# A mixture-of-experts layer on one core: another way to the first expert pair's tokens

## The chip, the cores and the metric

The kernel runs on one core of a Trainium2 chip. The metric is the device time of one execution in microseconds (us). Five engines work from queues of their own: TensorE (PE in the profile, its weight loads PEld), VectorE (DVE), ScalarE (ACT), GpSimd (POOL) and SyncE (SP), which here only issues DMAs. A wait at the head of a queue holds all that stands behind it.

## The reference

512 tokens of width 2048 go through one decoder layer in f32: normalisation, two attention groups, an output projection, and a mixture of experts. Only the last part matters here:

```python
def hierarchical_moe(h, router_g, router_e, w_gate, w_up, w_down):
    """h (N,D). Top-1 expert group, then top-2 experts inside the group."""
    pg = jax.nn.softmax((h @ router_g).astype(jnp.float32), axis=-1)
    ...
    top_p, top_i = lax.top_k(jax.nn.softmax(le, axis=-1), EXPERT_TOPK)
    gate = g_w[:, None] * top_p / jnp.sum(top_p, axis=-1, keepdims=True)
    expert = g_idx[:, None] * EXPERTS_PER_GROUP + top_i.astype(jnp.int32)
    ...
        u = jax.nn.silu(xe @ w_gate[e]) * (xe @ w_up[e])
        return u @ w_down[e]
    ...
    return jnp.zeros_like(h).at[buf_tok].add(yb * buf_w[:, None].astype(h.dtype))
```

There are 32 experts; each has three matrices of 4 MB (2048 x 512). Every token goes to two of them.

## The kernel before

All code is unrolled, and each engine's instructions stand in the order in which the Python code writes them; nothing reorders them. The first half of the kernel (to about 900 us) is the attention and the output projection. Its last steps are in `main_o`: for the last column block (c = 3) each of four groups of 128 tokens (t) is summed (`add_up`), turned and squared (`turn`: the copy `x1T` and the sum of squares `jk`), and multiplied with the router's weights (`route`). `keep` stores a block of the result `x1` to `x1d` in DRAM. `rs` and `r2` are the norm of each token.

Then comes the routing, mostly on VectorE with tokens on the partitions: `lgt` are the router's results, `first_max` finds the group and the two experts, M holds one-hot rows over 32 experts, and the matmuls `pos` count for each token its place in each expert. `key` is 512 times the expert plus the place, `gt` the two gate weights. `make_row` turns a column of 128 x 4 numbers into a row over 512 tokens on all partitions (four matmuls into a PSUM bank and a copy by ScalarE to `rows` or `more`); keys, `r2` and the gates are needed in that form.

The experts go in 16 pairs; an expert has 64 places, so that a pair fills 128 partitions. `find` compares the rows of keys with the keys of a pair's 128 places, which gives the one-hot matrix oT, and by products with `toki` (token numbers, loaded by GpSimd's queue) and `rrow` the token's number and norm for each place. GpSimd then gathers the tokens from `x1d` into xg by an indirect DMA; a place without a token has a number beyond the table, and its row is left as it was (xg is cleared once). `normed` scales xg, `turn_x` turns a quarter of it (four transposes on TensorE, four activations with scale and bias on ScalarE) into xe. A pair then multiplies with w_gate (g, four quarters of 16 matmuls), w_up (u) and w_down (y); an expert's weights come as four loads a matrix. `combine` adds the results to the tokens in the next pair's time. `find` for pair n + 1 stands ahead of pair n's g.

What sets the order of the loads: all large tiles come from one pool of 23 buffers (`slot`), handed out in the order of the code. SyncE issues the loads in order; `load_to(n)` issues up to item n, and a load waits until its buffer's last reader is done. Ahead of the first pair `load_to(n_phase1 + 12)` is called, so that 12 expert weights have buffers ahead of `rows`, `more`, two xg and xe; a thirteenth takes the router's buffer, and the next ones those of the first pair's weights as g uses them.

Of the kernel before, what the change touches and what calls it, by code (L numbers as in the profile page):

```python
# [34 lines left out]
C_ID, C_US, C_CM, C_SK, C_EI, C_D8, C_D4 = 0, 128, 256, 384, 400, 432, 440  # L35
NC_ = 444
# [41 lines left out]
def tile_hybrid_layer(ctx: ExitStack, tc, A, out, dbg=None):  # L78
# [891 lines left out]
    def main_o(c, q, h, start, stop):  # L970
# [9 lines left out]
        for t in range(4):  # L980
# [7 lines left out]
            if (c, q, h) == (3, 3, 1):  # L988
                add_up(c, t, pm, V)
                if t:  # L990
                    turn(c, t - 1)
                if t > 1:
                    route(c, t - 2)
            yield
        if stop:
            if c == 3:
# [5 lines left out]
                keep(c)  # L1002
# [67 lines left out]
    load_to(n_phase1 + 12)  # L1070
# [54 lines left out]
    M = k2([P, 3, 4, 32], "M")  # L1125
    for i, oh in enumerate((oh1, oh2)):
        V.tensor_tensor(M[:, i].rearrange("p t (g e) -> p t g e", g=4),
                        ohg[:, :, :, None].to_broadcast([P, 4, 4, 8]),
                        oh[:, :, None, :].to_broadcast([P, 4, 4, 8]), op=OP.mult)
# [17 lines left out]
    rows = slot([P, 4, S], name="rows")  # L1147
    more = slot([P, 2, S], name="more")
    rrow, toki = more[:, 0], more[:, 1]
    G.dma_start(toki, A["toki"])  # L1150

    def make_row(dst, col):

        pb = bank("at", "rows")
        for t in range(4):
            mm(pb[:, 128 * t:128 * t + 128], col[:, t:t + 1].to_broadcast([P, P]), ident, True, True)
        act(dst, pb)

    make_row(rows[:, 0], key[:, 0])
    make_row(rows[:, 1], key[:, 1])  # L1160
    make_row(rrow, r2)
# [13 lines left out]
    xg = [slot([P, D], name=f"xg{i}") for i in range(2)]  # L1175
    for t in xg:
        G.memset(t, 0.0)


    def find(sk, xs):  # L1180


        oT = k2([P, S], "oT", F32R)
        g = sm.tile([P, 6], F32, name="gs", tag="gs", bufs=3)
        gi = sm.tile([P, 1], I32, name="gi", tag="gi", bufs=3)
        t1 = sm.tile([P, S], F32, name="t1", tag="tmp", bufs=3)
        V.tensor_scalar(t1, rows[:, 0], sk, None, op0=OP.is_equal)
        V.scalar_tensor_tensor(oT, rows[:, 1], sk, t1, op0=OP.is_equal, op1=OP.add)
# [22 lines left out]
    def turn_x(xe, xs, c):  # L1211
# [45 lines left out]
    def need(i, k, e, c):  # L1257
        load_to(base + i + 1 + AH)
# [225 lines left out]
```

## Time and profile before

| | us |
|---|---|
| median of three executions | 1916.92 (1915.95 to 1920.93) |
| the profiled execution, its own time | 1916.49 |
| its span, first to last instruction | 1914.7 |
| TensorE busy | 1749.3 (91%) |
| VectorE busy | 973.1 (51%) |
| ScalarE busy | 602.1 (31%) |
| GpSimd busy | 393.2 (21%) |

The span is shown in 40 slices of 47.9 us, and the DMA engines' rate in them changes in the 20th: 374 GB/s in the 19th, 183 in the 20th, then 415 to 420 in each slice up to the 39th. A busy TensorE is no sign of its being the limit, since its matmuls count as busy while they stand in its pipeline. The chain that ended last is DMA for 42% of the span, w_u, w_d and w_g in turn.

### The profile page before, as it was taken

How to read it: one execution, taken by the hardware profiler on the slowest of the kernel's cores; microseconds unless marked ns; L12 is line 12 of the kernel's file. 1: busy time of each engine (PE TensorE's matmuls, PEld its weight loads, DVE VectorE, ACT ScalarE, POOL GpSimd, SP SyncE). 2: the span in 40 equal slices, each digit the busy share in tenths (PEclk: the TensorE clock that was granted, in tenths of full speed). 3: DMA queues.
4: the chain of work that ended last, by engine and by line, in shares of the span. 5: the costliest groups of instructions: out<-in, count | busy, mean ns of one | idle time of the engine just before them, and what ended most of it. 6: DMA issues, size and time to landing. Idle time of an engine off the chain costs nothing.

```text
span 1914.7 us, 21344 instructions
## 1 busy us (share of the span) xinstructions
PE 1749.3 (91%) x8098; PEld 982.9 (51%) x8098; DVE 973.1 (51%) x1473; ACT 602.1 (31%) x1138; POOL 393.2 (21%) x307
## 2 busy tenths in 40 slices
PE   4999999988899998897799999999999999999997
PEld 1777777765676676785433333333334333333333
DVE  6889722489846578768223243323333343323335
ACT  3655444554457534343221101211021101211020
POOL 3533311342436336665000000000000000000000
PEclk9999999999999999999899999999999999999999
DMA  9878312323235647679499999999999999999997
GB/s 350 278 267 293 132 66 88 132 89 110 89 105 225 222 158 272 255 287 374 183 420 419 419 419 419 419 419 420 419 419 419 419 420 419 419 419 419 419 415 284
DMA packets 136426, 585.06 MB, mean 306 GB/s; under 512 B 10760, under 2 KB 43696, under 8 KB 78976
## 3 DMA queue, kind: packets, MB, share of 16 engines
q1 hardware_dynamic: 132240, 569.09, 75.4%
q0 software_dynamic: 4080, 14.57, 2.1%
q8 instruction: 65, 1.06, 0.2%
q14 instruction: 41, 0.34, 0.0%
HBM read 583.60 MB, written 8.40 MB: 309 GB/s over the span
## 4 chain that ended last, share of the span: by engine, by line
DMA 42%; PE 8%; DVE 1%; issue 0%; ACT 0%; SPq 0%; DVEq 0%
DMA w_u<-in_w_up 17%; DMA w_d<-in_w_down 13%; DMA w_g<-in_w_gate 12%; PE y L103 3%; PE u L103 3%; PE g L103 1%; PE cb L103 1%; DVE x L1237 1%; PE ga L1215 1%; DMA xg<-x1d,gi 0%; DVE xg L1209 0%; DVE u L1272 0%; PE uT L1278 0%; DVE yt L1227 0%; DVE yL L1229 0%
## 5 line engine op out<-in xcount | busy, mean ns | idle before, releaser
L103 PE MATMUL u<-w_u,xe 128*64 128x512 f32 x1024 | 272.8, 617 | 29.9 <-DMA w_u<-in_w_up 29.2
L1237 DVE TENSOR_TENSOR x<-cb,x 128x512 f32<-128x512 f32 x256 | 157.2, 680 | 194.5 <-PE cb L103 194.5
L103 PE MATMUL g<-w_g,xe 128*64 128x512 f32 x1024 | 240.5, 597 | 14.5 <-DMA w_g<-in_w_gate 14.4
L103 PE MATMUL y<-w_d,uT 128*64 128x512 f32 x1024 | 236.9, 600 | 0.7 <-ACT uT L100 0.7
L1193 POOL DMA_INDIRECT xg<-x1d,gi x16 | 16.1, 1004 | 874.4 <-DVE t L1196 632.7
L282 POOL TENSOR_TENSOR accv<-accv,w_m_None 128x768 f32<-128x768 f32 (+2 forms) x62 | 153.0, 2468 | 207.7 <-ACT w_m_None L100 123.6
L103 PEld LDWEIGHTS u<-w_u,xe 128*64 128x64 f32 x1024 | 80.8, 140 | 211.0 <-issue 138.8
L103 PEld LDWEIGHTS g<-w_g,xe 128*64 128x64 f32 x1024 | 76.1, 137 | 168.0 <-issue 133.4
L1227 DVE SCALAR_TENSOR_TENSOR yt<-y,gs,accv 128x512 f32<-128x512 f32 x64 | 47.8, 747 | 202.4 <-PE y L103 202.4
L280 DVE SCALAR_TENSOR_TENSOR accv<-w_m_None,sil,accv 128x1280 f32<-128x1280 f32 (+2 forms) x62 | 134.8, 2174 | 5.9 <-issue 5.4
L100 ACT ACTIVATE xe<-ga,modc 128x128 f32<-128x128 f32 x256 | 94.5, 465 | 119.5 <-PE y L103 92.6
L103 PEld LDWEIGHTS y<-w_d,uT 128*64 128x64 f32 x1024 | 66.6, 136 | 116.0 <-issue 107.9
L100 ACT ACTIVATE uT<-uT 128x512 f32<-128x512 f32 x16 | 9.6, 598 | 358.7 <-PE uT L1278 358.7
L103 PE MATMUL cb<-yH,oT 128*128 128x512 f32 x256 | 107.8, 421 | 0.9 <-DVE x L1237 0.9
L100 ACT ACTIVATE yH<-yt 128x512 fp32r<-128x512 f32 x64 | 40.3, 630 | 204.6 <-DVE yt L1227 121.5
L103 PE MATMUL cb<-yL,oT 128*128 128x512 f32 x256 | 101.1, 395 | 0.0
L1229 DVE TENSOR_TENSOR yL<-yt,yH 128x512 fp32r<-128x512 f32 x64 | 44.3, 692 | 110.4 <-PE g L103 58.1
L394 DVE TENSOR_TENSOR hl<-w_O,hl 128x1024 fp32r<-128x1024 f32 x32 | 67.8, 2121 | 42.3 <-ACT hl L100 31.7
L1272 DVE TENSOR_TENSOR u<-sg,u 128x512 f32<-128x512 f32 x16 | 11.0, 688 | 127.9 <-PE u L103 127.9
L282 POOL TENSOR_TENSOR acc<-acc,w_m 128x160 f32<-128x160 f32 x105 | 61.2, 583 | 70.6 <-ACT w_m L100 62.9
L103 PEld LDWEIGHTS cb<-yH,oT 128*128 128x128 f32 x256 | 48.2, 188 | 50.0 <-issue 39.1
L1215 PEld LDWEIGHTS ga<-cst,xg 128*128 128x128 f32 x256 | 36.8, 210 | 64.3 <-issue 43.5
(413 smaller groups left out, 3168.7 us busy)
## 6 DMA issues: line engine op xcount, KB each, us to landing
w_g<-in_w_gate SPq DMA_DIRECT2D x128, 1024.0 KB, 19.9
w_u<-in_w_up SPq DMA_DIRECT2D x128, 1024.0 KB, 21.2
w_d<-in_w_down SPq DMA_DIRECT2D x128, 1024.0 KB, 19.9
w_m_None<-in_w_mod SPq DMA_DIRECT2D x64, 1024.0 KB, 4.9
w_m<-in_w_mod SPq DMA_DIRECT2D x32, 1024.0 KB, 10.7
w_B<-in_w_in SPq DMA_DIRECT2D x48, 512.0 KB, 4.6
w_O<-in_w_out SPq DMA_DIRECT2D x16, 1024.0 KB, 5.3
w_A<-in_w_in SPq DMA_DIRECT2D x8, 848.0 KB, 11.6
```

The costliest lines, as they stand in the source:

```text
L100: return SC.activation(o, i, f, **kw)
L103: return T.matmul(o, l, r, start=start, stop=stop, skip_group_check=skip)
L280: V.scalar_tensor_tensor(acc[:, lo], w[:, lo], s, acc[:, lo], op0=OP.mult, op1=OP.add)
L282: G.tensor_tensor(acc[:, hi], acc[:, hi], w[:, hi], op=OP.add)
L394: low_eng[0].tensor_tensor(t[:, 1], s, t[:, 0].bitcast(F32), op=OP.subtract)
L1193: G.indirect_dma_start(xs, None, x1d[:, :], bass.IndirectOffsetOnAxis(ap=gi[:, 0:1], axis=0), bounds_check=S - 1, oob_is_err=False)
L1215: T.transpose(pb[:, 128 * j:128 * j + 128], xs[:, 512 * c:512 * c + 512].rearrange("p (k j) -> p j k", j=4)[:, j], ident)
L1227: V.scalar_tensor_tensor(yt, y, g, rowv[G2][:, cs], op0=OP.mult, op1=OP.mult)
L1229: V.tensor_tensor(yL[:, cs], yt, yH[:, cs].bitcast(F32), op=OP.subtract)
L1237: return lambda: V.tensor_tensor(acc[q][:, t], pb, acc[q][:, t], op=OP.add)
L1272: V.tensor_tensor(u, sg, pb, op=OP.mult)
```

## The change

The first pair finds its tokens in another way. The sum of the one-hot rows over both choices, Mu, is made first, in bf16; `pos` is five bf16 matmuls. From the place in experts 0 and 1 a one-hot matrix `ohk` is made with tokens on the partitions and the 128 places along columns, and four matmuls with `tokv` (the token number in two parts, `r2` in three bf16 parts) give number and norm for each place. The gather goes in two halves of 1024 columns. M, the keys, the gates and the rest of the routing stand behind it.

The five rows (two keys, r2, two gates) are made by TensorE before the first g and stay in five PSUM banks; `make_rows` copies them out after g's activation, together with the load of `toki` and the clearing of xg1. There the buffers of `rows`, `more` and xg1 are taken. 16 expert weights are loaded ahead, and for the first eight steps the lead is 14. `find` and the gates of the first pair's time stand ahead of u. The first pair's quarters are turned one by one ahead of the products of g that use them, the first quarter by ScalarE and VectorE half each. The last block of x1 is stored in four pieces as it is made, and for the last 128 tokens the sum of squares goes ahead of the copy.

```diff
 def main_o(c, q, h, start, stop):
...
                 add_up(c, t, pm, V)
+                keep(c, t)
                 if t:
...
-                keep(c)
...
-        act(x1T[t], pt)
         jk = sm.tile([P, S], F32, name="jk", tag="tmp", bufs=3)
-        act(jk, x1[c][:, t], AF.Square, accum_out=ssx[:, t, c:c + 1])
+        if (c, t) == (3, 3):
+            act(jk, x1[c][:, t], AF.Square, accum_out=ssx[:, t, c:c + 1])
+            act(x1T[t], pt)
...
+            xg = [slot([P, D], name="xg0")]
+            G.memset(xg[0], 0.0)
...
-    load_to(n_phase1 + 12)
+    load_to(n_phase1 + 16)
...
+    spread_out(Mu, ohu)
     pp = bank("at", "pos")
-    mm(pp[:, :128], ustrict, M[:, 2].rearrange("p t e -> p (t e)"), True, False, True)
+    mm(pp[:, :128], identb, Mu.rearrange("p t e -> p (t e)"), True, False, True)
     for u in range(4):
-        mm(pp[:, 32 * u + 32:160], ones, M[:, 2, u:u + 1].to_broadcast([P, 4 - u, 32]), False, u == 3, True)
+        mm(pp[:, 32 * u + 32:160], oneb.to_broadcast([P, P]), Mu[:, u:u + 1].to_broadcast([P, 4 - u, 32]), False, u == 3,
+           True)
...
+    V.scalar_tensor_tensor(pm0, Mu[:, :, 0:2], float(-AWAY), pos[:, :, 0:2], op0=OP.mult, op1=OP.add)
+    ohk = sm.tile([P, 4, 2, 64], BF, name="ohk", tag="tmp", bufs=3)
+    V.tensor_tensor(ohk, cst[:, None, None, C_K:C_K + 64].to_broadcast([P, 4, 2, 64]),
+                    pm0[:, :, :, None].to_broadcast([P, 4, 2, 64]), op=OP.is_equal)
+    pf = bank("at", "first")
+    for t in range(4):
+        mm(pf[:, 0:5], ohk[:, t].rearrange("p e k -> p (e k)"), tokv[:, t], t == 0, t == 3)
...
+    for k in range(2):
+        G.indirect_dma_start(xg[0][:, HALF * k:HALF * k + HALF], None, x1d.rearrange("t (k n) -> (t k) n", k=2),
...
-    rows = slot([P, 4, S], name="rows")
-    more = slot([P, 2, S], name="more")
...
-    xg = [slot([P, D], name=f"xg{i}") for i in range(2)]
-    for t in xg:
-        G.memset(t, 0.0)
...
+    def turn_first(xe, xs):
+
+        for h, eng in enumerate((SC, V)):
+            pb = bank("at", f"ga{h}")
...
+                if h:
+                    V.tensor_scalar(xe[:, k], pb[:, s], a2[:, k:k + 1], sh2[:, k:k + 1], op0=OP.mult, op1=OP.add)
+                else:
+                    act(xe[:, k], pb[:, s], AF.Identity, bias=sh2[:, k:k + 1], scale=a2[:, k:k + 1])
...
-        load_to(base + i + 1 + AH)
+        load_to(base + i + 1 + (14 if i < 8 else AH))
...
-    oT, g = find(slotk[:, 0:1], xg[0])
-    make_row(rows[:, 2], gt[:, 0])
-    make_row(rows[:, 3], gt[:, 1])
+    g = g0
+    row_ps = [bank("mm", f"row{i}") if i < 4 else bank("at", "row4") for i in range(5)]
...
     for c in range(4):
         normed(xg[0], g, slice(512 * c, 512 * c + 512))
-        turn_x(xe, xg[0], c)
+    turn_first(xe, xg[0])
...
+                if (k, c) == (("g", 0) if n else ("u", 0)):
+                    if n == 0:
+                        rows, rrow, toki = make_rows()
+                        oT = match(slotk[:, 0:1])
+                    gate = gates(slotk[:, n:n + 1], g)
+                    if not last:
+                        after = find(slotk[:, n + 1:n + 2], xg[(n + 1) % 2])
+                if n == 0 and k == "g" and c < 3:
+                    turn_x(xe, xg[0], c + 1)
```

On VectorE, what leads to the first gather. Before, the end of the routing (gt) stands ahead of find, whose passes over rows end in the cast to gi, the gather's index (21 more instructions from M to the first gt row are left ahead of these):

```order
L1171 TENSOR_TENSOR gt<-scratch 128x4
L1172 TENSOR_TENSOR gt<-scratch 128x4
L1187 TENSOR_SCALAR t_6487<-rows,cst 128x512
L1188 SCALAR_TENSOR_TENSOR oT<-rows,cst,t_6487 128x512
L1190 SCALAR_TENSOR_TENSOR t_6490,gs<-oT,more 128x512
L1191 TENSOR_SCALAR gs<-gs 128x1
L1192 CAST gi<-gs 128x1
```

In the change the same engine goes from Mu to gi like this:

```order
L1144 TENSOR_TENSOR Mu<-scratch 128x128
L1157 CAST tokv<-r_4771 128x4
L1158 TENSOR_TENSOR scratch<-r_4771,tokv 128x4
L1159 CAST tokv<-scratch 128x4
L1160 TENSOR_TENSOR scratch<-scratch,tokv 128x4
L1161 CAST tokv<-scratch 128x4
L1163 SCALAR_TENSOR_TENSOR scratch<-Mu,pos 128x8
L1165 TENSOR_TENSOR ohk<-cst,scratch 128x512
L1172 COPY f_6455<-first 128x5
L1174 SCALAR_TENSOR_TENSOR gs<-f_6455 128x1 x2
L1175 CAST gi_6457<-gs 128x2
```

M, keys, gates and the whole of find have moved behind the cast.

On TensorE, the stretch ahead of the first pair's g (rows are the row matmuls, ga the transposes of xg, w_g the weights). Before:

```order
L103 MATMUL rows<-cst,key 128x128 x8
L103 MATMUL rows<-cst,r_4769 128x128 x4
L103 MATMUL rows<-cst,gt 128x128 x8
L1215 MATMUL ga<-cst,xg_6479 128x128 x16
L103 MATMUL g<-w_g_0_6231,xe 64x512
L103 MATMUL g<-w_g_0_6260,xe 64x512
```

In the change:

```order
L103 MATMUL row_6511<-cst,gt 128x128 x4
L1263 MATMUL ga_6536<-cst,xg_6275 128x128 x2
L1263 MATMUL ga_6541<-cst,xg_6275 128x128 x2
L1252 MATMUL ga<-cst,xg_6275 128x128 x4
L103 MATMUL g<-w_g_0_6236,xe 64x512
L103 MATMUL g<-w_g_0_6265,xe 64x512
L103 MATMUL g<-w_g_0_6236,xe 64x512
L103 MATMUL g<-w_g_0_6265,xe 64x512
L103 MATMUL g<-w_g_0_6236,xe 64x512
L103 MATMUL g<-w_g_0_6265,xe 64x512
L103 MATMUL g<-w_g_0_6236,xe 64x512
L103 MATMUL g<-w_g_0_6265,xe 64x512
```

Half of the 16 transposes stand ahead of the first matmul of g; the other two quarters have moved in between its quarters.

On GpSimd's queue, from the last sum of the modulation on. Before:

```order
L1024 DMA x1d<-x_3_5961 128x4x512
L1150 DMA more<-in_toki 128x512
L1177 MEMSET xg_6479 128x2048
L1177 MEMSET xg_6480 128x2048
L1193 DMA xg_6479<-x1d,gi 128x2048
```

In the change:

```order
L1077 MEMSET xg_6275 128x2048
L1032 DMA x1d<-x_3_5963 128x512 x4
L1178 DMA xg_6275<-x1d,gi_6457 128x1024 x2
L1352 DMA more<-in_toki 128x512
L1356 MEMSET xg_6629 128x2048
```

One clearing has moved ahead of the stores, the other, with toki's load, behind the first gather.

## Rows read from the trace of the kernel before

**Rows 1.** Stretches: length, engines busy (instructions), granted clock, DMA share, GB/s.

```profile
875.00:912.00 37.00, 27.78 (x131) 22.36 (x132) 26.08 (x43) 7.89 (x17) 12.82 (x7) 0.91 1.01 421
912.00:926.00 14.00, 10.04 (x48) 7.61 (x47) 6.25 (x28) 4.47 (x9) 0.81 (x1) 0.74 0.03 11
926.00:939.00 13.00, 7.66 (x32) 4.66 (x34) 5.93 (x17) 6.54 (x18) 1.29 (x2) 0.74 0.23 64
939.00:947.00 8.00, 8.00 (x40) 2.67 (x38) 0.00 (x0) 0.48 (x1) 0.00 (x0) 1.00 0.81 288
1043.00:1883.00 840.00, 788.86 (x3324) 305.82 (x3324) 293.25 (x536) 128.37 (x291) 12.96 (x13) 0.99 1.01 418
```

**Rows 2.** Waits of SyncE's queue, 888 to 945 us: total, times, longest.

```profile
SPq L256 <- PE g L103: 39.7, 2, 37.1
```

**Rows 3.** Timeline of SyncE, 939 to 940 us: start, length, instruction.

```profile
939.26 0.80 SPq L256 DMA_DIRECT2D w_u<-in_w_up  x2
```

**Rows 4.** Chain that ended last, 780 to 1060 us: start, length, what.

```profile
925.19 5.47 DMA xg<-x1d,gi
...
931.34 3.66 PE ga L1215 x16
935.00 14.53 PE g L103 x64
949.53 13.79 PE u L103 x64
...
967.43 0.68 PE ga L1215 x4
...
982.80 19.57 DMA w_u<-in_w_up
```

**Rows 5.** Timeline of TensorE, where g of pairs 1 and 2 begins.

```profile
982.60 10.47 PE L103 MATMUL g<-w_g,xe 128*64 128x512 f32 x48
...
1039.36 7.89 PE L103 MATMUL g<-w_g,xe 128*64 128x512 f32 x34
```

**Rows 6.** Timeline of ScalarE, the last sum of squares.

```profile
900.53 0.62 ACT L100 ACTIVATE jk<-x 128x512 f32<-128x512 f32 x1
```

**Rows 7.** Timeline of VectorE, 902 to 931 us; in brackets idle time before, and releaser.

```profile
902.44 1.84 DVE L158 TENSOR_SCALAR rt<-rt 128x4 f32<-128x4 f32 x1
...
904.57 0.31 DVE L1077 TENSOR_TENSOR lgt<-router,r 128x144 f32<-128x144 f32 x1
...
909.89 0.29 DVE L1130 TENSOR_TENSOR M<-M 128x128 f32<-128x128 f32 x1
912.67 0.29 DVE L1138 TENSOR_TENSOR posE<-pos,cst 128x128 f32<-128x128 f32 x1 [2.49 <-PE pos L103]
...
919.52 0.17 DVE L1099 TENSOR_REDUCE scratch<-scratch 128x4 f32<-128x16 f32 x1 [5.21 <-ACT scratch L100]
...
921.96 0.48 DVE L1187 TENSOR_SCALAR t<-rows,cst 128x512 f32<-128x512 f32 x1
...
924.18 0.15 DVE L1192 CAST gi<-gs 128x1 int32<-128x1 f32 x1
...
930.75 1.67 DVE L1209 TENSOR_SCALAR xg<-xg,gs 128x512 f32<-128x512 f32 x4 [5.81 <-DMA xg<-x1d,gi]
```

**Rows 8.** Timeline of GpSimd: the clearings and the first gather.

```profile
900.68 3.56 POOL L1177 MEMSET xg<- 128x2048 f32 x2
925.19 1.09 POOL L1193 DMA_INDIRECT xg<-x1d,gi  x1 [20.94 <-DVE t L1196]
```

**Rows 9.** Tile x1d, its stores and all gathers: from issue to landing.

```profile
DMA to landing us min/median/max: 5.5/8.9/11.8
```

**Rows 10.** DMA queues, 908 to 910 us (q1 SyncE's, q0 GpSimd's): packets, MB, share.

```profile
q1 hardware_dynamic: 80, 0.53, 63.2%
q0 software_dynamic: 78, 0.32, 38.8%
```

**Rows 11.** Stretch of 5 us as g begins; columns as in rows 1.

```profile
930.00:935.00 5.00, 3.66 (x18) 3.36 (x20) 4.18 (x11) 2.52 (x8) 0.00 (x0) 0.50 0.02 5
```

More of the change, by code (lines that the diff above doesn't have):

```diff
@@ L34 @@
 NV = 134
-C_ID, C_US, C_CM, C_SK, C_EI, C_D8, C_D4 = 0, 128, 256, 384, 400, 432, 440
-NC_ = 444
+C_ID, C_US, C_CM, C_SK, C_EI, C_D8, C_D4, C_K, C_T = 0, 128, 256, 384, 400, 432, 440, 444, 508
+NC_ = 516
 AWAY = 4096
@@ L1124, in tile_hybrid_layer, with spread_out @@
     first_max(oh2, m2, p8, d8, 8, "fm2")
[L1125 to L1128, printed above, removed]
+    ohu = part([P, 4, 8])
+    V.tensor_tensor(ohu, oh1, oh2, op=OP.add)
+    M, Mu = k2([P, 2, 4, 32], "M"), sm.tile([P, 4, 32], BF, name="Mu")
+    def spread_out(o, oh):
+        V.tensor_tensor(o.rearrange("p t (g e) -> p t g e", g=4), ohg[:, :, :, None].to_broadcast([P, 4, 4, 8]),
@@ new lines, in tile_hybrid_layer @@
+    pos = pp[:, :128].rearrange("p (t e) -> p t e", t=4)
+    ra, rb_ = part([P, 4]), part([P, 4])
+    V.tensor_copy(tokv[:, :, 2], r2)
+    V.tensor_tensor(ra, r2, tokv[:, :, 2], op=OP.subtract)
+    V.tensor_copy(tokv[:, :, 3], ra)
+    V.tensor_tensor(rb_, ra, tokv[:, :, 3], op=OP.subtract)
+    V.tensor_copy(tokv[:, :, 4], rb_)
+    pm0 = part([P, 4, 2])
+    V.scalar_tensor_tensor(pm0, Mu[:, :, 0:2], float(-AWAY), pos[:, :, 0:2], op0=OP.mult, op1=OP.add)
+    ohk = sm.tile([P, 4, 2, 64], BF, name="ohk", tag="tmp", bufs=3)
@@ L1135, in tile_hybrid_layer @@
+    V.tensor_copy(gi0, g0[:, 0:2])
+    HALF = D // 2
+    for k in range(2):
+        G.indirect_dma_start(xg[0][:, HALF * k:HALF * k + HALF], None, x1d.rearrange("t (k n) -> (t k) n", k=2),
+                             bass.IndirectOffsetOnAxis(ap=gi0[:, k:k + 1], axis=0), bounds_check=2 * S - 1,
+                             oob_is_err=False)
+    V.tensor_tensor(g0[:, 2:3], f5[:, 2:3], f5[:, 3:4], op=OP.add)
+    V.tensor_tensor(g0[:, 2:3], g0[:, 2:3], f5[:, 4:5], op=OP.add)
     while deferred:
@@ L1136, in tile_hybrid_layer @@
         later_run()
+    for i, oh in enumerate((oh1, oh2)):
+        spread_out(M[:, i], oh)
     posE = sm.tile([P, 4, 32], F32, name="posE", tag="tmp", bufs=3)
-    V.tensor_tensor(posE, pp[:, :128].rearrange("p (t e) -> p t e", t=4),
+    V.tensor_tensor(posE, pos,
                     cst[:, None, C_EI:C_EI + 32].to_broadcast([P, 4, 32]), op=OP.add)
@@ L1146, in tile_hybrid_layer @@
     V.tensor_copy(cnt, pp[:, 128:160])
-    rows = slot([P, 4, S], name="rows")
-    more = slot([P, 2, S], name="more")
[L1149 to L1161, printed above, removed]
     zg, gt = exps(pg, gl, mg, 4, "zg"), st([P, 2, 4], "gt")
@@ L1288, in tile_hybrid_layer, with make_rows @@
     xe = slot([P, 16, P], name="xe")
-    oT, g = find(slotk[:, 0:1], xg[0])
-    make_row(rows[:, 2], gt[:, 0])
-    make_row(rows[:, 3], gt[:, 1])
+    g = g0
+    row_ps = [bank("mm", f"row{i}") if i < 4 else bank("at", "row4") for i in range(5)]
+    for pb, col in zip(row_ps, (key[:, 0], key[:, 1], r2, gt[:, 0], gt[:, 1])):
+        for t in range(4):
+            mm(pb[:, 128 * t:128 * t + 128], col[:, t:t + 1].to_broadcast([P, P]), ident, True, True)
     for c in range(4):
         normed(xg[0], g, slice(512 * c, 512 * c + 512))
-        turn_x(xe, xg[0], c)
+    turn_first(xe, xg[0])
+    def make_rows():
+        rows, more = slot([P, 4, S], name="rows"), slot([P, 2, S], name="more")
+        G.dma_start(more[:, 1], A["toki"])
+        for dst, pb in zip((rows[:, 0], rows[:, 1], more[:, 0], rows[:, 2], rows[:, 3]), row_ps):
+            act(dst, pb)
+        xg.append(slot([P, D], name="xg1"))
+        G.memset(xg[1], 0.0)
+        return rows, more[:, 0], more[:, 1]
     done = iter(())
```

40 lines of the change are left out of this document (30 added, 10 removed).

## The prediction

> **What bounds the kernel now.** I read the stretches first, then SyncE's waits, then the engines between 900 and 940 us. From 1043 us to 1883 us the DMA engines are full at 418 GB/s [rows 1]: that is the expert weights, 384 loads of 1.05 MB, and each microsecond in which they do not flow is a microsecond of the end. They are full from 875 us on (421 GB/s), but not between 912 and 947 us: 11 GB/s for 14 us, 64 for 13, 288 for 8. Against 421 that is 13.6 + 11.0 + 2.5 = **27.2 us lost**. Bytes are the same before and after, so the gain is 27.2 us less what is lost afterwards.
>
> Why they stand still: SyncE's queue waited 37.1 us for TensorE's g [rows 2]. Thirteen loads fill all free buffers; the fourteenth takes the buffer of the first g weight, and is issued at 939.26 [rows 3], when the first quarter of g (64 matmuls in 14.53 us, 0.227 each, [rows 4]) has used it. So the path is: routing on VectorE, the gather, turning, a quarter of g. The chain view goes that way until 982.80 and along DMA from there. TensorE would be faster than the loads: pair 1 goes from 982.60 to 1039.36 [rows 5], 56.8 us, for 25.2 MB that take 59.8 us at 421 GB/s, and a gather besides.
>
> **The change part by part.** *Norm of the last block.* The sum of squares jk is made ahead of the copy x1T, not behind it (900.53 us, [rows 6]). It starts 1.2 us earlier, but the two ACT steps behind it now queue behind x1T: I take 0.85 of a possible 0 to 1.2.
>
> *The clearing.* A TENSOR_SCALAR of four elements takes 1.84 us at 902.44 [rows 7]; it ends at 904.28, the two clearings of xg on GpSimd at 904.24 [rows 8]. Both are moved, xg0's into a stretch before 890 where GpSimd has nothing left, xg1's behind the first g. With 0.16 us for it, about what the cast at 924.18 takes, 1.68 is saved; lgt starts at 904.57 - 2.53 = 902.0. The page "SBUF — State Buffer" of the Trainium skill ("SBUF: two separate sides") has an exclusive lock on a port pair that VectorE and GpSimd share; the rows agree. By that rule xg1's clearing would hold VectorE again at its new place, beside the second pair's search.
>
> *The search.* From lgt to the last M: 904.57 to 910.18, 5.61 us. One spread and one sum of 32 columns replace two spreads and a sum: 0.25 less; Mu is there at 907.35. TensorE's pos took 2.49 us in ten f32 passes [rows 7]; five bf16 ones aren't in the trace. Bounds are nothing and 2.5; I take 0.8, somewhat under half, since the passes are half as many, and VectorE covers up to 1.0 of it with five small steps on r2's parts (0.2 each): 908.35. Then key difference 0.2, one-hot columns 0.7 (512 columns, as the products in the old search), four bf16 matmuls 0.6 (0.2 to 2.5), copy 0.2, two sums 0.35: the index cast starts at 910.4. Before: 924.18, behind the keys, the rows, their evacuations (VectorE idle 5.21 us before 919.52), the gates and three passes over rows. So 13.8 us earlier; the gather goes from 925.19 to 911.4.
>
> The work that stood ahead is now behind: M, keys, gates. Between 912.67 and 921.96 it took 4 us without the 5.21, so gt is there at 916 to 917 and TensorE's 20 row matmuls by about 919, beside the gather. They stand ahead of the first transposes; if gt came after 919, they would be the new wait.
>
> *Three more loads.* Leaving rows, more and xg1 unallocated frees buffers: 16 loads go before g, and the last ones wait for the O products and the last sum, near 898 us. So DMA has work until 912.4 + (3 x 1.05 + 0.7 gathered - 0.26 toki)/0.421 = **920.9 us**. The gather is at most 0.83 MB by its stretch in [rows 1]; I take 0.7. xg0 takes the buffer of the fourth load early; loads 4 to 12 each go one release later, under a queue that was full then: 0.
>
> *The gather.* The last block of x1d is stored in four pieces, the last issued near 899.1; the longest landing in the trace is 11.8 us [rows 9], that store's, so 911 at the latest: no wait at 911.4, but little cover. Where both queues work, they move packet for packet (80 and 78 at 908 to 910, [rows 10]). The gather's halves go in alternation with the weights until these end: first half near 918.5, second with the last byte, 921.3. Bounds: 916.9 (the 5.5 us of an undisturbed gather) and 924.2 (11.8 us from the second issue). The page "DMA: Bandwidth & Descriptors" of the Trainium skill ("Rules for kernel authors") speaks against halves: small transfers should be made into one. Its fixed 2.0 us paid twice in a row would put the second half at about 923 and the kernel at 1898.5 us, inside the forecast's band (an estimate from that page); no row here splits a gather.
>
> *Landing to first release.* Before: 930.66 (925.19 + 5.47, [rows 4]) to 939.26, 8.6 us. Now the first half's products wait only for the first half. Behind the second landing: two scalings of 0.42 (1.67 for four, [rows 7]), which stand on VectorE ahead of the two turned blocks (0.25 each, estimated from the 0.42 of 512 columns), four matmuls 0.9, SyncE 0.65 as before (939.26 less 935.00 + 3.63), hops 0.2: 3.1. First release at **924.4**. The other quarters' transposes (0.68) now stand between the quarters of g, so it releases two buffers each 4.3 us, still faster than two loads of 2.5.
>
> *Restart.* From 939.26 the old kernel lost another 2.5 us until 947. The same here: 924.4 + 2.5 - 920.9 = 6.0 us lost.
>
> *Thin covers.* The last two g buffers go to rows and more, the first of u to xg1, so load 23 waits for u's first quarter (3.45 us), and 24 and 25 for its second. Laid out from 924.4, loads come 0.1 to 0.4 us late at three places. The second pair's search must follow g's end (935.9), five ACT copies (3.0), toki's landing, 5.6 us of VectorE and 1.8 in which the clearing may hold it: gather at 946.5, landed at 955.4 with the middling 8.9 us; TensorE comes to its transposes at 953.8 and waits 3 us. Loads are then covered for some 2 us behind it. I take 1.5 us for all, 0 to 4.
>
> Sum: lost 6.0 + 1.5 = 7.5; gain 27.2 - 7.5 = 19.7. The profiled execution took 1916.49 us (span 1914.7 and 1.8 around it), 0.4 under the median: **1896.8 us**. What follows the last load is not changed.
>
> **The rivals.** *Gap closed.* The gather is served at once: second half at 916.9, release at 920.0, lost 1.6 + 0.5: 1891.5, up to 1894.5. For it: an undisturbed landing of 5.5 us. Against: 9.5 us of queued loads are still under way at 911.4.
>
> *Late release.* The second half lands at 924.2, or g's first quarters run at the lower of TensorE's two levels, 1.2 GHz: the clock was 0.50 at 930 to 935 us after idle time [rows 11], with g starting then. The first release costs 0.9 more, its successors up to 3.6 each. Landing 924.2 + 3.1 + 0.9 + 2.5 - 920.9 = 9.8, covers 4: 13.8 lost, 1903; from 1899.5 to 1905.
>
> *Gain given back.* Pair 0 waits for row matmuls or xg1 by some 10 us more than laid out, at TensorE's cost, with all buffers held: lost 17 to 27, 1906 to 1916.
>
> *Slower.* The second pair's tokens: TensorE stands in y's first quarter until xg1 has landed, ten buffers behind it. That is a net loss only if the landing comes after about 976 us instead of 955.4, and slower by 0.3% from 982. toki and the gather at 11.8 each would give 965 and 1905, so something the trace doesn't show would have to come in; at 985 it would give 1925.
>
> *It doesn't do what it says.* If the gather waited for another store or for key rows, it would go at the old time with 16 loads in place: 1916.5 less 7.5 = 1909.
>
> **How the numbers follow.** Forecast (1894.5 to 1899.5) 0.57; gap closed 0.13; late release 0.20; given back or not done as said 0.06 (half of it above 1911); slower 0.04. A measurement tells about 0.3% from no change, 5.7 us: faster is below 1911.2. Faster 0.93, same 0.03, slower 0.04. The range leaves out the last cases and the outer tips of the others: 1892 to 1905.
>
> **What would show it.** Right: SyncE's long wait for g shrinks from 37 us to 24 or so, since the seventeenth load is asked for at 900 and issued near 924.4; POOL's first gather near 911.4; the DMA stretch 912 to 921 full and 921 to 927 nearly empty; full again by 930; the TENSOR_SCALAR at 0.16. Wrong: a DMA hole after 940, TensorE waiting over 6 us for xg at y, a gather issued after 915, or the hole of 6 us at 10 or more.

## The result and the profile after

| | before | after |
|---|---|---|
| median of four executions, us | 1918.49 (1915.95 to 1920.93) | 1898.55 (1895.36 to 1901.42) |
| ratio after to before | | 0.9898 (95%: 0.9883 to 0.9913) |
| profiled execution, its time | 1916.49 | 1895.36 |

0.9898 of 1916.9 is 1897.4 us; forecast were 1896.8, between 1892 and 1905. The profiled execution is the quickest of the four, and its 21.1 us are not all due to the change: its last sum of x1, which no edit moves, begins 3.4 us sooner than in the trace of before (ScalarE's first x1T copy of the last block at 890.00, against 893.42), and in another trace of the same kernel (below) it comes 4.0 us later again. Distances below are therefore counted from the issue of the first gather, and times are compared by ratios.

Stretches of the kernel after: length, engines busy (instructions), granted clock, DMA share, GB/s.

```profile
912.00:918.00 6.00, 3.14 (x25) 2.80 (x24) 1.58 (x7) 0.39 (x2) 0.00 (x0) 1.00 1.02 418
918.00:921.00 3.00, 2.23 (x11) 0.58 (x9) 1.04 (x3) 1.84 (x6) 0.00 (x0) 1.00 0.31 124
921.00:924.00 3.00, 2.79 (x14) 1.24 (x16) 0.48 (x2) 0.13 (x1) 0.00 (x0) 1.00 0.00 0
924.00:927.00 3.00, 3.00 (x16) 0.86 (x12) 0.00 (x0) 1.38 (x4) 0.00 (x0) 1.00 0.94 325
927.00:930.00 3.00, 3.00 (x16) 1.33 (x16) 0.00 (x0) 1.85 (x5) 0.00 (x0) 1.00 1.03 410
```

The hole that was 912 to 947 [rows 1] is now 918.9 to 925. I measure it in each trace in the same way: for each microsecond from 20 before to 60 after the first gather's issue, what is missing to 421 GB/s, as a share of that microsecond, summed (a microsecond over 421 counts against it). Before that is 27.1 us, after 7.6 (0.6 until 10 us after the issue, 5.9 in the next ten, 1.2 later). 19.5 us less lost; the ratio says 19.5.

SyncE's waits, 888 to 945 us (total, times, longest), and its next issue:

```profile
SPq L256 <- PE g L103: 29.2, 3, 22.3
```

```profile
923.18 0.81 SPq L256 DMA_DIRECT2D w_d<-in_w_down  x2
```

The wait of 37.1 us [rows 2] is one of 22.3. VectorE, GpSimd and TensorE of the kernel after (start, length, instruction, idle time before it and what ended it):

```profile
897.99 0.17 DVE L158 TENSOR_SCALAR rt<-rt 128x4 f32<-128x4 f32 x1
903.60 0.29 DVE L1144 TENSOR_TENSOR Mu<-scratch 128x128 bf16<-128x128 f32 x1
904.70 0.15 DVE L1163 SCALAR_TENSOR_TENSOR scratch<-Mu,pos 128x8 f32<-128x8 bf16 x1
906.41 0.17 DVE L1175 CAST gi<-gs 128x2 int32<-128x2 f32 x1
916.50 0.88 DVE L1246 TENSOR_SCALAR xg<-xg,gs 128x512 f32<-128x512 f32 x2 [3.70 <-DMA xg<-x1d,gi]
919.96 0.88 DVE L1246 TENSOR_SCALAR xg<-xg,gs 128x512 f32<-128x512 f32 x2 [2.57 <-DMA xg<-x1d,gi]
920.75 0.72 DVE L1268 TENSOR_SCALAR xe<-ga,modc 128x128 f32<-128x128 f32 x2
939.32 1.38 DVE L1216 TENSOR_SCALAR t<-rows,cst 128x512 f32<-128x512 f32 x1
```

```profile
907.43 1.09 POOL L1178 DMA_INDIRECT xg<-x1d,gi  x1 [10.95 <-DVE posE L1188]
938.61 1.81 POOL L1356 MEMSET xg<- 128x2048 f32 x1 [2.61 <-PE u L103]
943.77 1.05 POOL L1230 DMA_INDIRECT xg<-x1d,gi  x1 [3.36 <-DVE t L1233]
```

```profile
917.09 0.72 PE L1263 MATMUL ga<-cst,xg 128*128 128x128 f32 x4 [2.26 <-DVE xg L1246]
918.47 1.94 PE L103 MATMUL g<-w_g,xe 128*64 128x512 f32 x8 [0.18 <-ACT xe L100]
921.22 1.94 PE L103 MATMUL g<-w_g,xe 128*64 128x512 f32 x8 [0.81 <-DVE xe L1268]
954.95 0.72 PE L1252 MATMUL ga<-cst,xg 128*128 128x128 f32 x4 [2.00 <-DVE xg L1246]
```

What answers to rows 7 and 8: the index is cast at 906.41 and the gather issued at 907.43, in place of 924.18 and 925.19, the small TENSOR_SCALAR takes 0.17 us for 1.84, and the two halves have landed when VectorE's scalings begin, 9.0 and 12.4 us after the first issue. TensorE waits 2.00 us in y for the second pair's tokens.

### The profile page after: what moved, and what is told of

Its sections match the earlier page's. It is cut to its first block, busy times and chain, and to the rows that moved or that the text cites. A ratio compares the mean times of both kernels' runs of the same rounds, so it can differ in the third digit from the quotient of the medians.

```text
span 1893.6 us, 21355 instructions
## 1 busy us (share of the span) xinstructions
PE 1740.0 (92%) x8097; PEld 976.8 (52%) x8097; DVE 973.5 (51%) x1486; ACT 601.5 (32%) x1136; POOL 396.2 (21%) x311
## 2 busy tenths in 40 slices
DMA packets 136634, 585.09 MB, mean 309 GB/s; under 512 B 10866, under 2 KB 43802, under 8 KB 79270
## 4 chain that ended last, share of the span: by engine, by line
DMA 39%; PE 20%; DVE 6%; issue 4%; ACT 2%; POOL 1%; SPq 0%; DVEq 0%; POOLq 0%; ACTq 0%
DMA w_u<-in_w_up 15%; DMA w_g<-in_w_gate 12%; DMA w_d<-in_w_down 12%; PE O L103 5%; PE y L103 3%; PE u L103 3%; PE g L103 2%; PE B L103 2%; DVE hl L394 1%; PE cb L103 1%; DVE accv L280 1%; DVE x L1288 1%; PE z L103 1%; PE ga L1252 1%; DMA xg<-x1d,gi 1%
## 5 line engine op out<-in xcount | busy, mean ns | idle before, releaser
L103 PE MATMUL u<-w_u,xe 128*64 128x512 f32 x1024 | 265.8, 605 | 24.4 <-DMA w_u<-in_w_up 23.7
```

The costliest lines, as they stand in the source:

```text
L103: return T.matmul(o, l, r, start=start, stop=stop, skip_group_check=skip)
```

## Experiments

All edits are made to the changed kernel. "Lost" is the sum told of above; "release" is the issue of the seventeenth load (the fourteenth in e4), in us after the first gather's issue. Ratios are to the kernel before, with 95% intervals.

| kernel | halves landed | release | lost | ratio |
|---|---|---|---|---|
| changed kernel, first trace | 9.0, 12.4 | 15.75 | 7.6 | 0.9898 (0.9883 to 0.9913) |
| a0_again, the same | 9.2, 12.3 | 16.7 | 9.1 | 0.9912 (0.9894 to 0.9929) |
| e1_turn | 9.4, 12.5 | 16.8 | 9.2 | 0.9913 (0.9895 to 0.9931) |
| e3_small | 7.2, 8.5 | 12.9 | 6.3 | 0.9888 (0.9870 to 0.9905) |
| e8_both | 7.4; 9.4 or less | 13.1 | 5.4 | 0.9893 (0.9876 to 0.9909) |
| e2_one | 9.9 (whole) | 17.2 | 9.6 | 0.9921 (0.9904 to 0.9938) |
| e4_lead13 | 5.2 or less; 6.1 or less | 12.2 | 10.8 | 0.9908 (0.9892 to 0.9925) |
| e7_late | 6.0; 6.9 or less | 14.3 | 13.1 | 0.9928 (0.9912 to 0.9945) |
| e10_fill | 8.8, - | 15.7 | 10.0 | 0.9902 (0.9885 to 0.9918) |
| e5_allturn | 9.0, 12.1 | 20.3 | 11.4 | 0.9938 (0.9922 to 0.9955) |
| e6_memset | 8.5, 12.1 | 15.4 | 9.3 | 0.9904 (0.9888 to 0.9921) |
| e11_half | 7.6, 9.8 | 13.3 | 5.7 | 0.9902 (0.9882 to 0.9923) |

A landing is the start of the scaling that waited for it, less 0.09 us; "or less" where VectorE was busy when it came. 1916.5 less 27.1 plus "lost" gives each kernel's time (its ratio times 1916.9) within 3 us, but e5's (1900.8 for 1905.0). So the sum on which the forecast rests is the right one. A difference of 1 or 2 us is read from landings and releases: the ratios' intervals are wider than that, and "lost" has a spread of its own (e6_memset, whose path to the gather is 0.2 us longer than the changed kernel's and whose release comes 0.3 us sooner, lost 9.3 us for 7.6).

**a0_again**, the changed kernel beside the three next ones.

> The changed kernel once more, on the chip of the three next ones and in as many rounds, as their yardstick. In its first trace the gather's halves land 9.0 and 12.5 us after the first is issued, the seventeenth load goes 15.75 us after it, and the DMA engines lose 5.9 us between the end of the sixteen loads and full rate. Expected: the same distances within 0.3 us, and 0.988 to 0.991 of the kernel before.

The ratio is just outside what I expected, the release 0.9 us later, and the trace says why. TensorE in it, then its first quarter of g as a stretch:

```profile
921.32 0.72 PE L1263 MATMUL ga<-cst,xg 128*128 128x128 f32 x4 [2.71 <-DVE xg L1246]
922.70 5.35 PE L103 MATMUL g<-w_g,xe 128*64 128x512 f32 x16 [0.17 <-ACT xe L100]
```

```profile
922.70:928.00 5.30, 5.30 (x17) 1.43 (x17) 1.52 (x4) 1.37 (x4) 0.00 (x0) 0.68 0.06 22
```

The first half came 0.2 us later, TensorE stood idle for 2.71 us instead of 2.26, and while the first quarter of g ran the granted clock was 0.68 in the mean (0.50, which is 1.2 GHz, from 923.4 to 926.4), against 1.00 in the first trace. The quarter takes 5.35 us for 3.65, and the release comes 0.9 us later. That is the rival "late release", in one of the two traces of this kernel and not in the other.

**e1_turn**: VectorE's blocks of the first quarter ahead of the second half's scalings.

```diff
-    for c in range(4):
+    for c in range(2):
         normed(xg[0], g, slice(512 * c, 512 * c + 512))
     turn_first(xe, xg[0])
+    for c in range(2, 4):
+        normed(xg[0], g, slice(512 * c, 512 * c + 512))
```

> VectorE's two turned blocks stand ahead of the scalings of the second half, so that the first quarter of g hangs on the first half alone. Theory (the first release is held by VectorE's order behind the second landing): the blocks are ready near 10.7 us after the gather's issue, not 13.8, the seventeenth load goes near 13.5 us after it, not 15.75, the hole falls from 5.9 to 3.7 us, and the time by 2.2 us (0.9987 of the changed kernel). Rival (given back): the hole falls the same way, but the loads then wait for TensorE in the first pairs, whose chain the profile shows up to 1143 us, and the time stays.

```profile
921.28 0.73 DVE L1268 TENSOR_SCALAR xe<-ga,modc 128x128 f32<-128x128 f32 x2 [0.46 <-PE ga L1263]
922.99 0.88 DVE L1246 TENSOR_SCALAR xg<-xg,gs 128x512 f32<-128x512 f32 x2 [0.97 <-DMA xg<-x1d,gi]
```

```profile
920.52 0.72 PE L1263 MATMUL ga<-cst,xg 128*128 128x128 f32 x4 [2.88 <-DVE xg L1246]
921.90 5.35 PE L103 MATMUL g<-w_g,xe 128*64 128x512 f32 x16 [0.17 <-ACT xe L100]
```

The blocks begin 10.85 us after the issue and are ready at 11.6 (14.0 before), and g no longer waits for them. But the release is at 16.8: TensorE was idle for 2.88 us, and the first quarter ran at the lower clock. Both theories of the expectation fell. My sum was wrong too: the first quarter is 3.65 us of products, so that even at a clock of 1.00 the release would come at 15.1, not 13.5.

**e10_fill**: products that nobody needs in TensorE's idle time, written to the PSUM bank of `first`. The edit is not quite e1_turn and these products: it leaves out the two scalings of the second half (VectorE has two scalings of xg here and four in e1_turn), so the numbers that it computes for the first pair are not the reference's. Bytes (585.09 MB) are the same. The first quarter of g hangs on the first half alone, so its clock and the release can be set beside e1_turn's; time and "lost" can't.

```diff
-    for c in range(4):
+    for c in range(2):
         normed(xg[0], g, slice(512 * c, 512 * c + 512))
+    for _ in range(4):
+        mm(pf, ident, cst[:, 0:512], True, True, True)
     turn_first(xe, xg[0])
```

> The kernel with VectorE's two blocks ahead of the second half's scalings, and four idle products of 512 columns on TensorE between the row products and the first transposes, some 1.9 us, written to a bank that nobody reads. In that kernel TensorE was idle for 2.88 us there, the granted clock was 0.50 when g began, and its first quarter took 5.35 us. Theory (the clock fell for the idle time): granted clock 1.00, first quarter 3.65 us, the seventeenth load at 15.1 us after the gather's issue, not 16.8, hole 5.3 in place of 7.0, time 1.7 us less. Rival (the clock falls at times whatever TensorE does): first quarter 5.35 us again, and the release at 16.8 or, with the products late, more.

```profile
917.07 3.60 PE L103 MATMUL first<-cst 128*128 128x512 f32 x8
920.50 0.63 PE L1263 MATMUL ga<-cst,xg 128*128 128x128 f32 x4
921.79 3.65 PE L103 MATMUL g<-w_g,xe 128*64 128x512 f32 x16 [0.17 <-ACT xe L100]
```

```profile
921.80:925.40 3.60, 3.60 (x17) 1.07 (x17) 0.10 (x1) 1.36 (x4) 0.00 (x0) 1.00 0.01 2
```

Each product was two instructions, so they took 3.6 us, not 1.9, and held the transposes back by 1.2 us (920.50, 1.80 us behind the first scaling at 918.70; 0.58 in e1_turn). Even so the clock is 1.00, the quarter takes 3.65 us, and the release is at 15.7 instead of 16.8. So what TensorE did before counts, and not chance alone. All twelve traces of the changed kernel and its variants agree at this place: in the five in which TensorE had idled for 2.49 to 5.55 us ahead of the first transposes (e5_allturn, a0_again, e1_turn, e2_one, e7_late) the clock fell to 0.50 as g began, in the seven with 0 to 2.26 us it stayed at 1.00. But the length of the last idle time is not all: at the second pair's transposes a0_again waited 1.86 us and its clock fell, and the first trace, with its wait of 2.00 us there (above), kept 1.00. TensorE in a0_again, and a stretch behind it:

```profile
959.70 0.72 PE L1252 MATMUL ga<-cst,xg 128*128 128x128 f32 x4 [1.86 <-DVE xg L1246]
```

```profile
960.70:964.10 3.40, 3.40 (x10) 0.93 (x7) 0.00 (x0) 0.35 (x1) 0.00 (x0) 0.50 1.00 417
```

**e3_small, e11_half**: the last four loads ahead (13 to 16) in runs of 2 or 4 KB instead of 8. In e11_half the loop is over two halves of two.

```diff
-            else:
-                Q.dma_start(t, ap)
+            elif it[0] == "u" and it[1] < 2 and it[2] > 1:
+                for j in range(4):
+                    Q.dma_start(t[:, j], ap[:, j])
+            else:
+                Q.dma_start(t, ap)
```

> The last four of the sixteen loads ahead go as four DMAs each, with runs of 2 KB in place of 8. Theory (the gather's packets take turns with the weights', one for one, so that a big packet of the other queue is what a packet of 4 KB waits for): at 421/16 GB/s on each DMA engine eight turns of 4 + 8 KB are 3.7 us and of 4 + 2 KB 1.9, so the halves land near 7.2 and 9.0 us after the issue, not 9.0 and 12.5; the seventeenth load goes some 3.4 us earlier, the hole is 2.5 us, the time 3.4 us less (0.998 of the changed kernel). Rival (the gather lands when the bytes queued ahead of it are through): the landings stay at 9.0 and 12.5, and the time is the same or, if loads in small runs are slower, up to 2 us more.

> The last four loads ahead go as two DMAs each with runs of 4 KB (8 KB in the changed kernel, 2 KB in the kernel with four DMAs). By turns of packets, fitted to the two runs at hand (5.4 us and per half eight turns of 4 KB plus the other's run at 421/16 GB/s): halves at 7.8 and 10.3 us after the issue, between 7.2 and 8.5 of the 2 KB runs and 9.2 and 12.4 of the 8 KB runs; release near 13.7; the stretch ahead of the gather loses less than the 0.8 us that the 2 KB runs lost. Time between the two, 0.989 to 0.990. Rival (what counts is the number of DMAs or the later issue of the loads): near one of the two ends.

GpSimd's gather and VectorE's scalings in e3_small, then in e11_half:

```profile
909.85 1.09 POOL L1181 DMA_INDIRECT xg<-x1d,gi  x1 [10.96 <-DVE posE L1191]
917.14 0.88 DVE L1249 TENSOR_SCALAR xg<-xg,gs 128x512 f32<-128x512 f32 x2 [2.14 <-DMA xg<-x1d,gi]
918.44 0.88 DVE L1249 TENSOR_SCALAR xg<-xg,gs 128x512 f32<-128x512 f32 x2 [0.42 <-DMA xg<-x1d,gi]
```

```profile
909.78 1.09 POOL L1181 DMA_INDIRECT xg<-x1d,gi  x1 [10.96 <-DVE gs L1184]
917.43 0.88 DVE L1249 TENSOR_SCALAR xg<-xg,gs 128x512 f32<-128x512 f32 x2 [2.48 <-DMA xg<-x1d,gi]
919.67 0.88 DVE L1249 TENSOR_SCALAR xg<-xg,gs 128x512 f32<-128x512 f32 x2 [1.36 <-DMA xg<-x1d,gi]
```

The weights still to come at the gather's issue are the same in the changed kernel and in these two, 4.0 MB, yet the second half lands 12.1 to 12.5, 9.8 and 8.5 us after the issue with runs of 8, 4 and 2 KB (10.3 was expected for 4 KB, and 9.0 for 2 KB). The DMA queues from 4.5 to 7.5 us after the issue, in the first trace of the changed kernel, in e11_half and in e3_small (q1 SyncE's, q0 GpSimd's: packets, MB, share):

```profile
q1 hardware_dynamic: 126, 0.93, 74.6%
q0 software_dynamic: 119, 0.31, 26.3%
...
q1 hardware_dynamic: 196, 0.70, 59.1%
q0 software_dynamic: 186, 0.51, 43.7%
...
q1 hardware_dynamic: 347, 0.64, 57.6%
q0 software_dynamic: 229, 0.53, 46.9%
```

With 8 and 4 KB the packets of the two queues come about one for one, and GpSimd's bytes rise from 0.31 to 0.51 MB as the other queue's packets get shorter. In e11_half 0.7 MB of weights still come after the second half has landed. So beside a busy queue a gather does not wait until the bytes queued ahead of it are through; its packets take turns with the other queue's, and the length of that queue's runs sets its share. The Trainium skill's page "DMA: Bandwidth & Descriptors" ("Queues, rings and completion order") has the DMA engines go round the queues packet by packet; the rows with 8 and 4 KB agree, and these numbers are its price here.

With 2 KB it is no longer one for one (347 to 229), and 0.53 MB is hardly more than 0.51; the rest of what e3_small gains comes from an earlier start: from 3.0 to 4.2 us after the issue its gather moves 25 packets, those of the other two kernels none. SyncE waited for earlier loads of w_u here and issued nine of the sixteen short DMAs only behind the gather, so that less stood ahead of it; in e11_half it was one of eight, 0.6 us behind the gather's issue, and so well before the stretch above. That the runs count, and not the later issue of the loads, is shown by the rows of the changed kernel and e11_half, in which both queues have work throughout, and not by e3_small's landings.

With TensorE idle for 0.70 and 1.03 us only, the clock stays at 1.00. Runs of 2 KB cost something of their own: "lost" until 10 us after the issue is 1.3 with 2 KB (in e8_both too), but 0.8 with 4 KB lies within the 0.4 to 0.9 of the kernels with 8 KB and the same gather.

e3_small's median was 1895.83 us (1893.75 to 1897.61) beside 1901.09 (1896.72 to 1901.78) for the changed kernel in the same rounds. It is the best of the twelve; its interval and that of a0_again overlap, so that it beats the changed kernel is likely and not certain.

**e8_both**: e1_turn and e3_small together.

> Both edits of the two kernels before. If both theories hold: halves at 7.2 and 9.0 us, the seventeenth load 11.8 us after the gather's issue, a hole of no more than the 2.4 us that a load takes from its issue to full rate, time 3.5 to 4 us under the changed kernel (0.998). If only the order on VectorE counts: as that kernel, 2.2 us. If the time lost moves to the first pairs: as the changed kernel.

Release 13.1 as with short runs alone: once the halves land 1.3 us apart, as in e3_small, VectorE's order is hidden behind the first eight products of g. That theory of mine did not hold here either.

**e2_one**: the first gather in one piece.

```diff
-    for k in range(2):
-        G.indirect_dma_start(xg[0][:, HALF * k:HALF * k + HALF], None, x1d.rearrange("t (k n) -> (t k) n", k=2),
...
+    G.indirect_dma_start(xg[0], None, x1d[:, :], bass.IndirectOffsetOnAxis(ap=gi0[:, 1:2], axis=0),
+                         bounds_check=S - 1, oob_is_err=False)
```

> The first gather goes in one piece of 2048 columns; all else is the changed kernel, whose halves landed 9.0 to 9.4 and 12.3 to 12.5 us after the first issue. Theory (packets take turns): some 5.4 us and eight turns of 8 + 8 KB at 421/16 GB/s, 4.9 us, together 10.3 us for the whole: later than the first half, sooner than the second. Behind it stand four scalings and two blocks on VectorE; the seventeenth load goes 16.4 us after the issue at full clock and 17.5 if the clock has fallen (15.75 and 16.7 with halves), so the time is 0 to 1 us more. Rival (lands with the last byte queued, as I predicted): near 12.4, the load at 18.5, 2 us more. The Trainium skill's page DMA: Bandwidth & Descriptors (Rules for kernel authors), small transfers made into one: its 2.0 us once instead of twice would make the time 2 us less (an estimate from that page).

```profile
910.24 1.09 POOL L1177 DMA_INDIRECT xg<-x1d,gi  x1 [11.07 <-DVE posE L1186]
920.24 1.68 DVE L1244 TENSOR_SCALAR xg<-xg,gs 128x512 f32<-128x512 f32 x4 [4.95 <-DMA xg<-x1d,gi]
```

The whole lands 9.9 us after the issue (10.3 expected by turns): 0.5 to 0.9 us later than a first half, and 2.5 us sooner than a second. The rule of the Trainium skill's page "DMA: Bandwidth & Descriptors" ("Rules for kernel authors"), to make small transfers into one, agrees with this as far as the transfer goes. The end is no sooner: four scalings stand behind the landing, TensorE was idle for 3.51 us, the clock fell, and the release is at 17.2 against 16.7, with 0.9921 against 0.9912, which the intervals don't tell apart.

**e4_lead13**: thirteen loads ahead, as many as before.

```diff
-    load_to(n_phase1 + 16)
+    load_to(n_phase1 + 13)
+    rows, more = slot([P, 4, S], name="rows"), slot([P, 2, S], name="more")
+    xg.append(slot([P, D], name="xg1"))
+    for t in (rows[:, 0], more[:, 0], xg[1]):
+        G.memset(t[:, 0:1], 0.0)
...
-        load_to(base + i + 1 + (14 if i < 8 else AH))
+        load_to(base + i + 1 + AH)
```

> Thirteen loads ahead in place of sixteen: rows, more and xg1 get their buffers early (a clearing of one column holds them), the lead is 12 again; nothing else is undone. Rival (each load ahead is worth its 2.5 us, as I predicted): 7.5 us more, 0.995 of the kernel before. Theory (the loads ahead also slow the gather, so that a part comes back): the weights end near 4 us after the gather's issue, the halves land at 6.5 and 8, not 9.2 and 12.4; TensorE's row products end at 7.4, g starts at 9.2, the first release is at 13.0, the hole 11.3 us in place of 5.9 to 7.1: 4.2 to 5.4 us more, 0.9937.

```profile
911.94 1.09 POOL L1182 DMA_INDIRECT xg<-x1d,gi  x1 [10.76 <-DVE posE L1192]
917.25 1.67 DVE L1250 TENSOR_SCALAR xg<-xg,gs 128x512 f32<-128x512 f32 x4
920.50 3.65 PE L103 MATMUL g<-w_g,xe 128*64 128x512 f32 x16 [0.17 <-ACT xe L100]
924.18 0.80 SPq L256 DMA_DIRECT2D w_u<-in_w_up  x2
```

Three loads fewer, 7.5 us of transfer, and the time is the same within the intervals; "lost" is 1.7 us more than in a0_again. Where the rest went can be read: hardly anything queues beside the gather any more (0.9 MB), both halves are there when VectorE comes to them, the release is 4.4 us sooner, and from 30 us after the issue on 0.2 us is lost, not 1.6, in a kernel whose toki and xg1 are there early: 7.5 - 4.4 - 1.4 = 1.7. Against the first trace, in which the clock did not fall either, it is 3.2 us more, so the three loads and what goes with them are worth 1.7 to 3.2 us by the traces, and nothing that the ratios tell. Even my theory had put the loss too high, at 4.2 to 5.4.

**e7_late**: index and gather behind gt.

```diff
-    V.tensor_copy(gi0, g0[:, 0:2])
-    HALF = D // 2
-    for k in range(2):
-        G.indirect_dma_start(...)
...
     V.tensor_tensor(gt[:, 1], p2, den, op=OP.mult)
+    V.tensor_copy(gi0, g0[:, 0:2])
+    HALF = D // 2
+    for k in range(2):
+        G.indirect_dma_start(...)
```

> The first gather's index is cast and the gather issued behind gt, some 6.2 us later; nothing else is changed. If the gather's issue counts one for one (as I predicted): 6.2 us more, 0.9945 of the kernel before. Theory (a later gather competes with fewer loads): from the old point of issue the halves land at 14 and 15.5 (9.2 and 12.4 before), the first release at 18.9, or 20.6 if TensorE's clock has fallen meanwhile, in place of 15.75 to 16.7: 3 to 4 us more, 0.993.

```profile
919.53 1.09 POOL L1205 DMA_INDIRECT xg<-x1d,gi  x1 [17.27 <-DVE gi L1202]
925.61 1.67 DVE L1246 TENSOR_SCALAR xg<-xg,gs 128x512 f32<-128x512 f32 x4 [6.92 <-DMA xg<-x1d,gi]
928.08 5.71 PE L103 MATMUL g<-w_g,xe 128*64 128x512 f32 x16
```

The gather goes 6.3 us later (17.8 us after the last store of x1d, not 11.5) and its halves land within 6.0 and 6.9 us. The release moves from 16.7 to 20.6 after the old point of issue, as expected, and "lost" by 4.0 us. So a microsecond of the gather's issue is worth 0.6 here, not 1, beside a trace whose clock fell too; beside the first trace, whose clock did not, "lost" is 5.5 us more, and it is 0.9.

**e5_allturn**: all quarters turned ahead of g.

```diff
     turn_first(xe, xg[0])
+    for c in range(3):
+        turn_x(xe, xg[0], c + 1)
...
-                if n == 0 and k == "g" and c < 3:
-                    turn_x(xe, xg[0], c + 1)
```

> All four quarters of the first pair's tokens are turned ahead of g, as before the change; the rest is the changed kernel. If the interleaving brings what I put on it: g's first product waits for the last quarter, whose columns land 12.4 us after the gather's issue; g starts near 14.4, the seventeenth load goes near 18.1 in place of 15.75 to 16.7, 1.5 to 2.4 us more, 0.992 of the kernel before. Rival (the later quarters of g release their buffers each 3.65 us instead of 4.3, which pays it back): no difference.

```profile
925.31 15.82 PE L103 MATMUL g<-w_g,xe 128*64 128x512 f32 x64
930.86 17.49 SPq L256 DMA_DIRECT2D w_d<-in_w_down  x8
```

g starts 14.8 us after the issue (14.4 expected) and takes 15.82 us for its four quarters, the first of them longer, for the clock again. Release at 20.3, 2.3 us more lost than in a0_again, and the largest ratio of the set. By "lost" the interleaving is worth what it was given, 1.5 to 2.4; by the ratios it is some 5 us, with intervals that just overlap, and what makes the difference is not known.

**e6_memset**: two clearings where before had them.

```diff
-            G.memset(xg[0], 0.0)
...
     load_to(n_phase1 + 16)
+    for _ in range(2):
+        G.memset(xg[0], 0.0)
```

> Two clearings of xg0 behind the last store of x1d, where the kernel before had the two of its buffers (one of the two is idle work); nothing else is changed. Theory (a clearing on GpSimd holds certain VectorE instructions until it ends): the TENSOR_SCALAR of four elements ends with the second clearing and takes 1.8 to 2.0 us, not 0.17; all behind it, the gather's issue too, is 1.7 to 1.9 us later. If the issue counts one for one, as I predicted, the time is 1.8 us more; if a later gather is served faster, as the kernel with the late gather would say (4.0 us of release for 6.3 of issue), 1.1 us more. Rival (the stall before had another cause): 0.17 us, and no change.

```profile
897.20 1.82 POOL L1085 MEMSET xg<- 128x2048 f32 x1
898.73 0.33 DVE L158 TENSOR_SCALAR rt<-rt 128x4 f32<-128x4 f32 x1
```

0.33 us, not 1.8. The instruction ended at 899.06, when the first clearing did (899.02), and VectorE then had its turn ahead of the second. In the kernel before it came at 902.44, as the second clearing began, and got all of it [rows 7, 8]. In the changed kernel the second pair's t at 939.32 takes 1.38 us, where the like one at 936.30 takes 0.49, beside xg1's clearing. So the stall is there, one clearing at a time, and its price hangs on the moment: 0.2, 0.9 and 1.7 us in these three cases. The Trainium skill's page "SBUF — State Buffer" ("SBUF: two separate sides") says that the lock is held for the whole instruction; the rows agree.

## Why the prediction was right, point by point

In the frame of the trace of before (3.4 us added to the times after):

| step | forecast | measured |
|---|---|---|
| lgt | 902.0 | 901.9 |
| Mu ready | 907.35 | 907.3 |
| key difference (behind pos) | 908.35 | 908.1 |
| index cast | 910.4 | 909.8 |
| gather issued | 911.4 | 910.9 |
| first half, second half landed | 918.5, 921.3 | 919.8, 923.3 |
| sixteen loads through (918 to 921 us at 124 GB/s: 918.9) | 920.9 | 922.3 |
| first release | 924.4 | 926.6 |
| lost in the hole | 6.0 | 5.9 |
| lost by thin covers, and ahead of the gather | 1.5, 0 | 1.2, 0.6 |

**The path to the gather** held within 0.6 us. The unknown of it, pos in bf16, was hidden behind VectorE's five small steps, as was said: pos had ended 0.2 us before VectorE needed it.

**The clearing.** 1.67 us came back, as forecast, but my reading that the instruction waits for both clearings is only half of it (e6): it was the bad luck of the moment that made it 1.84.

**The gather** is the term that was mis-sized: the second half came 2.0 us later than taken, inside the bounds. I took it to land with the last byte queued, and here it did within 1 us (922.3 and 923.3), but that was luck: with runs of 4 KB it landed while 0.7 MB were still to come (e11). What sets it is turns of packets, so that the length of the other queue's runs counts.

**Three more loads** were right in their sum with the rest and wrong as a term. They were credited with 7.5 us and the earlier gather with 13.8, one for one. e4 and e7 show that neither is: 1.7 to 3.2 of the 7.5 are left when the loads are taken away, and 0.6 to 0.9 of each microsecond of the issue, because a gather that shares the DMA engines with fewer loads lands sooner. The forecast came out right because the landing had been worked out beside those loads, and by luck, because three errors cancel: the loads ended 1.4 us later than laid out (0.6 us were lost ahead of the gather, where I had put 0), the release came 2.2 later, and the DMA engines were back at full rate 1.6 us after it, counted as loss, where 2.5 had been taken.

**Landing to release** was 3.3 us for 3.1 in the first trace. In a0_again it was 4.4, for the clock. The rival "late release" was right about that mechanism and its price of 0.9 us, not about the successors: from 926.6 us on the clock was 1.00 again, the second quarter of g took 3.65 us, and the next fall came at the second pair's transposes.

**Thin covers**: TensorE's wait in y for the second pair's tokens was 2.0 us (3 taken), the gather was issued at 947.2 in the old frame (946.5) and landed 9.7 us later. No hole of the kind that the rival "slower" needed.

**The other rivals.** Gap closed needed the gather at once; only where few loads were left beside it did it land like that (e4 with thirteen loads, e7 with a late gather), and there the loads that would have used the time are missing or through. What the prediction wanted as signs of "wrong" (a hole after 940, over 6 us of waiting in y, a gather after 915, a hole of 10 us) did not appear. The spread between executions of one kernel, up to 10 us, is larger than all that is left to explain; 4 us of it are there before the last block of x1 is summed, and what makes them was not tried. Not tried alone either were pos in bf16, the search by one-hot columns, the order of the last sum of squares, the stores in pieces and the lead of 14: what is said of them is read from the traces of the whole change.

## What to carry to other kernels

Work that is loaded ahead to cover a small, urgent transfer competes with that transfer: price the two together, and test each alone before crediting it in full. If a gather has to come through a full queue, try shorter runs in the loads that it meets: bytes stay the same, and here the landing moved from 12.4 to 9.8 us with 4 KB and to 8.5 with 2 KB, and that the kernel's time gains by it (some 5 us by the medians of e3_small and a0_again) is likely, not certain. An engine that idles just ahead of the critical products can cost more than the order in which its inputs come.

## What the runs showed of the hardware that I had not expected

- A gather's landing beside full loads goes by the length of their runs: second half at 12.1 to 12.5, 9.8 and 8.5 us with 8, 4 and 2 KB (the last in part because fewer loads had been issued ahead of it), and in 6.9 at most where 1.3 MB of loads were left beside it (e7).
- TensorE idled for 2.71 us ahead of g in a0_again, and the granted clock then read 0.50; in the first trace of the same kernel it idled for 2.26 us, from 0.2 us of difference in a landing, and the clock read 1.00. The 16 products of the first quarter of g take 5.35 or 3.65 us. At the second pair's transposes 1.86 us were followed by 0.50 and 2.00 us by 1.00, so the last idle time alone does not tell.
- VectorE gets in between two clearings of GpSimd that stand back to back: a waiting TENSOR_SCALAR took 0.33 us in one place and 1.84 in another.
